# Attention layer 0 of a two-layer encoder: no stores issued from GpSimd, stores one tile later, squares of the softmax sums on ScalarE

## The chip, the cores and the metric

The kernel runs on one core of a Trainium2 chip. A core has five engines that run their own instruction queues side by side: TensorE (PE, matrix products), VectorE (DVE), ScalarE (ACT), GpSimd (POOL) and SyncE (SP, which here only issues DMAs). DMAs can be issued from SP, ACT or POOL. The metric is the device time of one execution in microseconds (us), lower is better.

## The reference

The trunk has 1024 tokens of width 1024 and two layers. Layer 0 is differential attention with 8 heads, layer 1 is multi-head latent attention. Only layer 0's attention is touched here:

```python
def block(qb):
    sc = jnp.einsum('bqhcd,bkhcd->bhcqk', qb, k, preferred_element_type=f32) * scale
    p = jax.nn.softmax(sc, axis=-1)
    p = p[:, :, 0] - lam * p[:, :, 1]
    return jnp.einsum('bhqk,bkhd->bqhd', p.astype(v.dtype), v)
o = _from_blocks(lax.map(block, _to_blocks(q)))
o = _rmsnorm(o, subln_g) * (1.0 - lambda_init)
o = o.reshape(b, s, DA_WIDTH) * jax.nn.silu(z)
return o @ w_out
```

For each head there are two softmaxes, their difference times V, an RMS norm over the 128 values of the head (the "sub-norm"), and a product with a gate silu(z). All is in float32.

## The kernel before

Every float32 product is made of three matrix products of rounded parts: an operand is split into a high part (ACT copies it to the type that TensorE reads) and a low part (DVE or POOL subtracts), and `mm3` issues high x high, high x low and low x high (L178 to L180).

**The stage.** Layer 0's attention runs over 8 heads, two halves of 512 query rows, and four tiles of 128 rows in each half: 64 tiles. For one tile `q_tile` makes two score matrices of 128x1024 (L1157), each with a maximum on DVE (L456) and an exponential with its sum on ACT (L458); the sums of the first softmax of four tiles stand in the four columns of `zz`. DVE then combines the two exponentials (L1163 to L1165). One to two tiles later PE transposes the result (L439), ACT and DVE split it (L441, L442), and `pv` multiplies it with V. Because the combined exponentials are not divided by the first softmax's sum, the sub-norm must know the square of that sum: `subln` (L1236) adds a multiple of `zz` squared to the mean square of the output before the inverse root.

**Work laid beside it.** Between the pieces of a tile `fill` steps a stream of other matrix products (the projections of the next heads, `gen_strips0`, written `acc`). By `FILL0` a tile has five such steps or three. After each step, and once more at the end of each tile, `side.tick()` runs the next entry of a queue of small jobs. A job of `rot_job` (L369) turns one half of a head's q or k by its position: POOL makes two products and a sum (`first_`, `second`, L390 to L394), ACT copies the high part and issues its store (`high`, L398 and L400), POOL makes the low part (`low`, L403), and the low part is stored. `None` entries in the queue space the steps out. `z_done` (L847) makes a gate and stores it.

**The sub-norm.** When a half of a head is through, `head_out` on ACT takes the squares and a scaled copy of the output out of PSUM, and `subln` multiplies by the gate on POOL (L1240). Its `rest` is put on a list, `hooks`, and runs at the end of the next tile (`after_scores` runs the hooks that were there before the tile's last `pv`). `rest` sums the squares with a matrix product against ones (L1247), then has four DVE instructions on 128x4 values (L1250 to L1253), an inverse root on POOL (L174) and a product on POOL (L1255). L1250 and L1252 read two operands from SBUF, L1253 one, L1251 one from SBUF and one from PSUM. `finish` then sends the four factors through DRAM so that they come back as a row on all partitions: a store (L1195), one tile later a load (L1199), one tile after that a product (L1202) and the store of the output (L1203). The store of L1195, that of L1203 and that of the low part (L405) are issued from POOL.

**What sets the order.** A planner arranges the instructions of each engine ahead of time from its own estimate of when each can start, so an instruction can stand on its engine well ahead of its place in the program: L1250, which needs only `zz`, runs before the matrix product that L1251 needs. `in_turn` keeps an instruction in the order of the program, which is done for all of POOL's work here; `behind` keeps one behind the latest instruction that matters on its engine. On the chip each engine works its list from front to back, and an instruction that waits holds those behind it. SP's list holds nearly all loads and stores.

**The end of the stage.** In head 7 the stream is used up, and the first products of the output projection take its place (`extra0`, L1613). They need the outputs of earlier heads from DRAM (`oF`), loaded by SP and split on ACT and POOL (L1518, L1519). The sub-norms of head 7 run from a list of their own, `rests`.

Of the kernel before, what the change touches and what calls it, by code (L numbers as in the profile page):

```python
# [15 lines left out]
AF = mybir.ActivationFunctionType  # L16
ALU = mybir.AluOpType
# [4 lines left out]
P = 128  # L22
# [5 lines left out]
NH = 8  # L28
QL = 384
KVL = 256  # L30
EPS = 1e-6
# [7 lines left out]
ROT = 2  # L39
# [33 lines left out]
GUARD = 2.0 ** 40  # L73
FMAX = 3.4028e38
# [5 lines left out]
def f32v(ap):  # L80
    return ap.bitcast(F32)
# [3 lines left out]
def trunk(ctx: ExitStack, tc: tile.TileContext, A, out):  # L85
    nc = tc.nc
    SP, PE, V, S, G = nc.sync, nc.tensor, nc.vector, nc.scalar, nc.gpsimd
# [47 lines left out]
    oF = [dr.tile([NH, 2, P, HF], F32, name=f"oF{l}") for l in range(2)]  # L135
# [3 lines left out]
    zS = dr.tile([NH, 2, P, HF], F32, name="zS")  # L139
    rS = [[[dr.tile([P, HF], F32, name=f"rS{k}{h}{f}") for f in range(2)] for h in range(NH)] for k in range(2)]  # L140
    hS = [[[dr.tile([2, P, HF], F32, name=f"hS{k}{h}{f}") for f in range(2)] for h in range(NH)] for k in range(2)]
# [29 lines left out]
    def rsqrt(w, n):  # L171

        y = sm.tile([P, n], F32, name="rq_y")
        G.tensor_tensor(out=y, in0=w, in1=mhalf[:, :n], op=ALU.pow)  # L174
        return y
# [9 lines left out]
    def behind(eng):  # L185

        return tc.issue_after(mk[eng]) if eng in mk else nullcontext()

    def in_turn(ins):

        return tc.keep_in_program_order(ins) if mk else ins
# [123 lines left out]
    side = Side()  # L315
# [53 lines left out]
    def rot_job(kind, h, half, eng, raw=None):  # L369

        cs = slice(half * HF, half * HF + HF)
        b = {"raw": raw}
        turn_ = in_turn if eng is G else lambda ins: ins

        def rpt(name):
            return wp.tile([P, HF], F32, name=name, tag="rp", bufs=6)

        def fetch():
            src = b["raw"]
            if src is None:  # L380
                src = rS[kind][h][half]
                b["raw"] = rpt("rp_raw")
                SP.dma_start(b["raw"], src)
            b["sw"] = rpt("rp_sw")
            for q in range(4):
                SP.dma_start(b["sw"][q * 32 : q * 32 + 32], src[(q ^ 1) * 32 : (q ^ 1) * 32 + 32])

        def first_():
            b["r"] = rpt("rp_r")
            turn_(eng.tensor_mul(b["r"], b["raw"], cosT[:, cs]))  # L390

        def second():
            turn_(eng.tensor_mul(b["sw"], b["sw"], sinT[:, cs]))
            turn_(eng.tensor_add(b["r"], b["r"], b["sw"]))  # L394

        def high():
            with behind("S"):
                cp = S.copy(b["sw"].bitcast(F32R), b["r"])  # L398
            with tc.issue_after(cp.ins):
                S.dma_start(hS[kind][h][half][0], b["sw"])  # L400

        def low():
            turn_(eng.tensor_sub(b["raw"].bitcast(F32R), b["r"], b["sw"]))  # L403
            if eng is G:
                in_turn(G.dma_start(hS[kind][h][half][1], b["raw"]))  # L405

        def store():
            if eng is not G:
                SP.dma_start(hS[kind][h][half][1], b["raw"])

        return fetch, first_, second, high, low, store

# [56 lines left out]
    def t3(ap_):  # L469
        return ap_.rearrange("p (t q) -> p t q", t=4)  # L470
# [173 lines left out]
    for f in range(2):  # L644
        fs = slice(f * HF, f * HF + HF)
        spread = PE.matmul(cb[:, fs], ones[0:1, :], crow[0:1, fs], start=True, stop=True).ins
# [158 lines left out]
        store_v(0, *((tp, acc, tt, fh, "tk", 16) if tt < V_LATE else (pg, acc, tt, fh, "ada", 2)))  # L805


    KS, QS, GZ = {}, {}, {}
    parked = []

    def silu_gate(tp, acc):
# [7 lines left out]
    def rot_done(kind, h):  # L819
        def f(acc, half):  # L820
            raw = wp.tile([P, HF], F32, name="rp_raw", tag="rp", bufs=6)
            if kind:
                S.copy(raw, acc)
            else:
                S.mul(raw, acc, SC0)
            fetch, *steps = rot_job(kind, h, half, G, raw)
            fetch()
            side.add(*[None] * ROT, *steps[:2], None, None, *steps[2:4])
        return f

    def load_k(h):
# [15 lines left out]
    def z_done(h):  # L847
        def f(acc, half):
            t = wp.tile([P, HF], F32, name="zth", tag="rp", bufs=6)
            S.activation(t, acc, AF.Tanh, scale=0.5)  # L850
            V.scalar_tensor_tensor(out=t, in0=t, scalar=1.0, in1=acc, op0=ALU.add, op1=ALU.mult)
            SP.dma_start(zS[h, half], t)
            if parked:
                fetch, *steps = rot_job(*parked.pop(0), G)
                side.add(fetch, None, None, *steps[:2], None, None, *steps[2:4])
        return f

    def load_gate(h, half):
# [332 lines left out]
    def finish(o, y, l, h, half, dst, ap_, dgs):  # L1191

        if dst is None and l == 0:
            d_ = dr.tile([HF], F32, name="bc_d", tag="bcd", bufs=4)
            in_turn(G.dma_start(d_.rearrange("(p t) -> p t", p=P), y))  # L1195

            def spread():
                b = ap_.tile([P, HF], F32, name="bc_s", tag="osq", bufs=4)
                SP.dma_start(b, d_[None, :].to_broadcast([P, HF]))  # L1199

                def scale():
                    in_turn(G.tensor_mul(t3(o), t3(o), b.rearrange("p (q t) -> p t q", t=4)))  # L1202
                    in_turn(G.dma_start(oF[l][h, half], o))  # L1203

                hooks.append(scale)

            hooks.append(spread)
            return
        if dst is None:
            b, rb = bcast_rows(ap_, y, "osq", 4)  # L1210

            def scale():
                in_turn(G.tensor_mul(t3(o), t3(o), rb))
                hooks.append(lambda: hooks.append(store))

            def store():
                SP.dma_start(oF[l][h, half], o)

            hooks.append(scale)
            return  # L1220
        rb = bank("z", "rb") if l else Y[1]
        for j in range(4):
            js = slice(j * P, (j + 1) * P)
            S.mul(dgs[:, js], ident, y[:, j : j + 1])
            PE.matmul(rb[:, js], ones, dgs[:, js], start=True, stop=True)
        V.tensor_mul(o, o, rb)
# [9 lines left out]
    def subln(o, sq, zz, half, h, dst):  # L1236


        if dst is None:
            in_turn(G.tensor_mul(o, o, GZ[h][half]))  # L1240
        else:
            V.tensor_mul(o, o, GZ[h][half])

        def rest():
            pt = Y[0] if dst is not None else ssq_at[0] if ssq_at else bank("acc", "ssq")
            for j in range(4):
                PE.matmul(pt[:, j : j + 1], sq[:, j * P : (j + 1) * P], ones[:, 0:1], start=True, stop=True)  # L1247
            w = sm.tile([P, 4], F32, name="sl_w")
            fin = sm.tile([P, 4], F32, name="sl_f")
            V.tensor_mul(fin, zz, zz)  # L1250
            V.scalar_tensor_tensor(out=w, in0=fin, scalar=P * EPS / GUARD ** 2, in1=pt[:, 0:4], op0=ALU.mult, op1=ALU.add)  # L1251
            V.scalar_tensor_tensor(out=fin, in0=fin, scalar=FMAX / GUARD ** 2, in1=w, op0=ALU.mult, op1=ALU.is_ge)  # L1252
            V.tensor_scalar(w, w, 3.0e38, None, op0=ALU.min)  # L1253
            y = rsqrt(w, 4)
            in_turn(G.tensor_mul(y, y, fin))  # L1255
            if dst is not None:
                return lambda: finish(o, y, 0, h, half, dst, None, sq)
            finish(o, y, 0, h, half, None, a0b, sq)

        if dst is None:  # L1260
            (hooks if h < NH - 1 else rests).append(rest)
        else:
            return rest()
# [28 lines left out]
            if kh == 1 and qp % 2 == 1:  # L1292
                c["close"](qp // 2, c["o_"], self.zz)

    tails, hooks = [None, None], []

    def run_tails(fill):

# [184 lines left out]
    class Seven:  # L1483
# [32 lines left out]
        def put(self, raw, hi, lo, eng):  # L1516
            with behind("S"):
                S.copy(hi, raw)  # L1518
            sub = eng.tensor_sub(lo, raw, f32v(hi))  # L1519
            if eng is G:  # L1520
                in_turn(sub)
                self.sub = sub.ins

        def fetch(self, n):
            for h in range(4):
                self.fetch_a(n, h)
                self.fetch_w(n, h)
# [319 lines left out]
    for n, rows, acc, f in ((3, 4, Z, 1), (4, 0, Z, 1), (5, 4, Y, 1), (6, 4, Y, 0)):  # L1847
# [5 lines left out]
        for i in range(4):  # L1853
# [24 lines left out]
            if i == 1 and n == 5:  # L1878
                raws = [[], []]
                with tc.issue_after(w6):  # L1880
                    for k, (tag, nb) in enumerate((("wraw", 2), ("gz", 3))):
                        for f in range(2):
                            raw = wst.tile([P, HF], F32, name="wraw", tag=tag, bufs=nb)
# [225 lines left out]
    for h in range(2):  # L2109
        w = strip1(6 + h)  # L2110
# [481 lines left out]
    def scale(tt, y):  # L2592
        full, early = xs_[tt], tt // 4
        c1, c2_ = halves[early], halves[1 - early]

        def second():
            V.scalar_tensor_tensor(out=full[:, c2_], in0=full[:, c2_], scalar=y, in1=fg[:, c2_], op0=ALU.mult, op1=ALU.mult)
            SP.dma_start(out[tt][:, c2_], full[:, c2_])

        def first_():  # L2600
            S.mul(full[:, c1], full[:, c1], y)
            SP.dma_start(out[tt][:, c1], full[:, c1])

        if tt == NT - 2:
            held.extend((second, first_))
        else:
            second()
            first_()
# [160 lines left out]
```

## Time and profile before

| what | us |
|---|---|
| median of 3 runs | 1430.9 |
| lowest, highest | 1430.05, 1431.73 |
| the profiled execution | 1429.41 |
| its span, from the first to the last instruction | 1427.6 |
| PE, DVE, ACT, POOL busy in it | 1374.6, 1027.2, 733.6, 729.7 |

The profiled execution takes 1429.41 us, of which 1427.6 lie between its first and its last instruction. The last head of the attention of layer 0 ends near 720 us on the span's own clock, and its 64 tiles begin near 220 us. PE's busy time counts the whole pipeline of a matrix product, so PE can be "busy" and still not work at its densest.

### The profile page before, as it was taken

How to read it: one execution, taken by the hardware profiler on the slowest of the kernel's cores; microseconds unless marked ns; L12 is line 12 of the kernel's file. 1: busy time of each engine (PE TensorE's matmuls, PEld its weight loads, DVE VectorE, ACT ScalarE, POOL GpSimd, SP SyncE). 2: the span in 40 equal slices, each digit the busy share in tenths (PEclk: the TensorE clock that was granted, in tenths of full speed). 3: DMA queues.
4: the chain of work that ended last, by engine and by line, in shares of the span. 5: the costliest groups of instructions: out<-in, count | busy, mean ns of one | idle time of the engine just before them, and what ended most of it. 6: DMA issues, size and time to landing. Idle time of an engine off the chain costs nothing.

```text
span 1427.6 us, 20963 instructions
## 1 busy us (share of the span) xinstructions
PE 1374.6 (96%) x7298; PEld 1143.4 (80%) x7298; DVE 1027.2 (72%) x1418; ACT 733.6 (51%) x1332; POOL 729.7 (51%) x600
## 2 busy tenths in 40 slices
PE   8998899999999999999899999999999999999997
PEld 6786678778878778888687788887888888888886
DVE  7699927998887878788777986744656555555684
ACT  5543314556655555665655653334454454555554
POOL 5424440556788685565686332533141263754773
PEclk9999999999999999999999999999999999999999
DMA  9845788777778767765484236488444355665373
GB/s 338 267 123 186 274 221 276 216 228 228 237 226 241 220 208 210 213 194 177 138 312 155 77 81 222 141 279 254 158 121 118 110 152 184 194 219 199 132 262 118
DMA packets 172604, 282.42 MB, mean 198 GB/s; under 512 B 21777, under 2 KB 58769, under 8 KB 172498
## 3 DMA queue, kind: packets, MB, share of 16 engines
q1 hardware_dynamic: 164290, 262.43, 58.9%
q0 software_dynamic: 3600, 10.26, 2.0%
q10 hardware_dynamic: 4608, 8.39, 1.6%
q8 instruction: 57, 0.93, 0.3%
q14 instruction: 49, 0.40, 0.1%
HBM read 182.49 MB, written 86.98 MB: 189 GB/s over the span
## 4 chain that ended last, share of the span: by engine, by line
PE 69%; DVE 13%; issue 5%; DMA 5%; POOL 4%; ACT 3%; SPq 1%; POOLq 0%; ACTq 0%; DVEq 0%
PE s L2383 10%; PE tr L439 6%; PE acc L178 6%; PE acc L180 6%; PE acc L179 6%; PE s L1157 5%; PE pv L178 3%; PE pv L179 3%; PE pv L180 3%; DVE ada L480 2%; DVE sl_f L1250 1%; PE oy L180 1%; PE vps L178 1%; PE oy L179 1%; PE vps L179 1%
## 5 line engine op out<-in xcount | busy, mean ns | idle before, releaser
L441 ACT CAST pth<-tr 128x512 fp32r<-128x512 f32 x256 | 150.5, 588 | 264.7 <-PE tr L439 262.1
L442 DVE TENSOR_TENSOR ptl<-tr,pth 128x512 fp32r<-128x512 f32 x256 | 176.0, 688 | 138.2 <-ACT pth L441 133.6
L456 DVE TENSOR_REDUCE nm<-s 128x1 f32<-128x1024 f32 x192 | 233.6, 1217 | 19.6 <-PE s L1157 10.4
L224 POOL TENSOR_TENSOR wl<-wraw,wh 128x512 fp32r<-128x512 f32 (+2 forms) x65 | 84.2, 1298 | 272.7 <-ACT wh L223 211.1
L458 ACT ACTIVATE e<-s,nm 128x1024 f32<-128x1024 f32 x128 | 143.6, 1122 | 70.5 <-DVE nm L456 70.0
L439 PE MATMUL tr<-ident,e 128*128 128x128 f32 x1024 | 156.7, 275 | 14.6 <-DVE ptl L442 14.3
L439 PEld LDWEIGHTS tr<-ident,e 128*128 128x128 f32 x1024 | 121.3, 141 | 58.4 <-DVE ptl L442 37.3
L178 PE MATMUL pv<-pth,vt 128*128 128x256 f32 x512 | 147.8, 289 | 0.0
L179 PE MATMUL pv<-ptl,vt 128*128 128x256 f32 x512 | 147.6, 288 | 0.0
L180 PE MATMUL pv<-pth,vt 128*128 128x256 f32 x512 | 145.1, 283 | 0.0
L178 PE MATMUL acc<-h0h,wh 128*128 128x512 f32 x264 | 109.5, 415 | 3.8 <-DVE zu L1054 3.4
L180 PE MATMUL acc<-h0h,wl 128*128 128x512 f32 x264 | 105.1, 398 | 0.6 <-POOL wl L224 0.6
L179 PE MATMUL acc<-h0l,wh 128*128 128x512 f32 x264 | 105.7, 400 | 0.0
L178 PEld LDWEIGHTS pv<-pth,vt 128*128 128x128 f32 x512 | 97.7, 191 | 3.0 <-ACT pth L441 0.4
L179 PEld LDWEIGHTS pv<-ptl,vt 128*128 128x128 f32 x512 | 98.1, 192 | 1.8
L180 PEld LDWEIGHTS pv<-pth,vt 128*128 128x128 f32 x512 | 98.1, 192 | 0.4
L1519 POOL TENSOR_TENSOR wol<-wol,woh 128x512 fp32r<-128x512 f32 x56 | 82.3, 1493 | 26.3 <-ACT woh L1518 23.7
L1157 PE MATMUL s<-ks,qa 128*128 128x512 f32 x256 | 85.8, 416 | 8.5 <-DVE e L1165 8.0
L1165 DVE SCALAR_TENSOR_TENSOR e<-s,z,e 128x1024 f32<-128x1024 f32 x64 | 82.2, 1284 | 2.1
L1157 PE MATMUL s<-ks,qb 128*128 128x512 f32 x256 | 83.5, 401 | 0.0
L458 ACT ACTIVATE s<-s,nm 128x1024 f32<-128x1024 f32 x64 | 70.0, 1093 | 8.5 <-DVE nm L456 8.1
L224 POOL TENSOR_TENSOR wl<-zraw,wh 128x512 fp32r<-128x512 f32 (+2 forms) x32 | 46.0, 1444 | 52.0 <-ACT wh L223 48.7
(496 smaller groups left out, 3653.1 us busy)
## 6 DMA issues: line engine op xcount, KB each, us to landing
ada<-in_ada_ss SPq DMA_DIRECT2D x32, 512.0 KB, 5.7
vt<-vS SPq DMA_DIRECT2D x32, 512.0 KB, 5.6
wol<-tS SPq DMA_DIRECT2D x56, 256.0 KB, 5.2
wraw<-in_w_s SPq DMA_DIRECT2D x52, 256.0 KB, 3.5
vS<-v_hl SPq DMA_DIRECT2D x26, 512.0 KB, 6.0
tS<-ob SPq DMA_DIRECT2D x48, 256.0 KB, 2.6
bc_s<-bc_d SPq DMA_DIRECT2D x34, 256.0 KB, 4.0
hS<-rp_sw ACTq DMA_DIRECT2D x32, 256.0 KB, 3.4
```

The costliest lines, as they stand in the source:

```text
L178: PE.matmul(psum, ah, bh, start=first, stop=False, skip_group_check=skip)
L179: PE.matmul(psum, ah, bl, start=False, stop=False, skip_group_check=skip)
L180: mm3.last = PE.matmul(psum, al, bh, start=False, stop=last, skip_group_check=skip).ins
L224: sub = (V if pair_of else G).tensor_sub(l_[:, :n], raw[:, :n], f32v(h_[:, :n]))
L439: transpose_p.last = PE.transpose(tr[:, j, :], p[:, kt * P : (kt + 1) * P], ident).ins
L441: mk["S"] = S.copy(pth[kh][:, :, dst], tr).ins
L442: mk["V"] = V.tensor_sub(ptl[kh][:, :, dst], tr, f32v(pth[kh][:, :, dst])).ins
L456: mk["V"] = V.reduce_max(nm, s_ps, axis=AX.X, negate=True).ins
L458: mk["S"] = S.activation(e, s_ps, AF.Exp, bias=nm, scale=1.0, accum_out=zs).ins
L1157: PE.matmul(s_ps[:, kc * HF : (kc + 1) * HF], src[:, c, ql], KS[h][kc][:, c, :], start=fst, stop=not fst)
L1519: sub = eng.tensor_sub(lo, raw, f32v(hi))
L2383: PE.matmul(s_ps[:, kc * HF : (kc + 1) * HF], lhs, rhs(kc), start=i == 0, stop=i == 4)
```

## The change

Four things are altered, all in layer 0.

- The low part of a turned half is stored by ACT instead of POOL when POOL made it, from an entry of its own in the side queue: two entries after the low part. The pause between `second` and `high` is one entry instead of two.
- The gate's store (heads 1 to 6) is put on `hooks` and so issued at the end of a later tile.
- `finish` for layer 0 goes in five steps: the factors' store from SP one tile after they are made (`put`), then as before load and product, and the output's store from SP one more tile later (`store`).
- In `rest` the two squares of `zz` are made on ACT, with their factors inside the square; the limit of 3e38 is put on the matrix product's sum before the addition; the guard compares with the matrix product's sum in PSUM. Two DVE instructions stay, each with one operand in PSUM.

```diff
         def low():
             turn_(eng.tensor_sub(b["raw"].bitcast(F32R), b["r"], b["sw"]))
-            if eng is G:
-                in_turn(G.dma_start(hS[kind][h][half][1], b["raw"]))
 
         def store():
-            if eng is not G:
-                SP.dma_start(hS[kind][h][half][1], b["raw"])
+            (S if eng is G else SP).dma_start(hS[kind][h][half][1], b["raw"])
...
             fetch, *steps = rot_job(kind, h, half, G, raw)
             fetch()
-            side.add(*[None] * ROT, *steps[:2], None, None, *steps[2:4])
+            side.add(*[None] * ROT, *steps[:2], None, *steps[2:4], None, steps[4])
...
-            SP.dma_start(zS[h, half], t)
+            if 0 < h < NH - 1:
+                hooks.append(lambda: SP.dma_start(zS[h, half], t))
+            else:
+                SP.dma_start(zS[h, half], t)
             if parked:
                 fetch, *steps = rot_job(*parked.pop(0), G)
-                side.add(fetch, None, None, *steps[:2], None, None, *steps[2:4])
+                side.add(fetch, None, None, *steps[:2], None, *steps[2:4], None, steps[4])
...
         if dst is None and l == 0:
             d_ = dr.tile([HF], F32, name="bc_d", tag="bcd", bufs=4)
-            in_turn(G.dma_start(d_.rearrange("(p t) -> p t", p=P), y))
+            rb = []
+
+            def put():
+                SP.dma_start(d_.rearrange("(p t) -> p t", p=P), y)
+                hooks.append(spread)
 
             def spread():
                 b = ap_.tile([P, HF], F32, name="bc_s", tag="osq", bufs=4)
                 SP.dma_start(b, d_[None, :].to_broadcast([P, HF]))
-
-                def scale():
-                    in_turn(G.tensor_mul(t3(o), t3(o), b.rearrange("p (q t) -> p t q", t=4)))
-                    in_turn(G.dma_start(oF[l][h, half], o))
-
+                rb.append(b.rearrange("p (q t) -> p t q", t=4))
                 hooks.append(scale)
 
-            hooks.append(spread)
+            def scale():
+                in_turn(G.tensor_mul(t3(o), t3(o), rb[0]))
+                hooks.append(store)
+
+            def store():
+                SP.dma_start(oF[l][h, half], o)
+
+            hooks.append(put)
             return
...
-            V.tensor_mul(fin, zz, zz)
-            V.scalar_tensor_tensor(out=w, in0=fin, scalar=P * EPS / GUARD ** 2, in1=pt[:, 0:4], op0=ALU.mult, op1=ALU.add)
-            V.scalar_tensor_tensor(out=fin, in0=fin, scalar=FMAX / GUARD ** 2, in1=w, op0=ALU.mult, op1=ALU.is_ge)
-            V.tensor_scalar(w, w, 3.0e38, None, op0=ALU.min)
+            S.activation(w, zz, AF.Square, scale=math.sqrt(P * EPS) / GUARD)
+            S.activation(fin, zz, AF.Square, scale=1.0 / GUARD)
+            V.scalar_tensor_tensor(out=w, in0=pt[:, 0:4], scalar=3.0e38, in1=w, op0=ALU.min, op1=ALU.add)
+            V.scalar_tensor_tensor(out=fin, in0=fin, scalar=FMAX, in1=pt[:, 0:4], op0=ALU.mult, op1=ALU.is_ge)
             y = rsqrt(w, 4)
             in_turn(G.tensor_mul(y, y, fin))
```

The list `hooks` is only made earlier in the program (L808 instead of L1295).

More of the change, by code (lines that the diff above doesn't have):

```diff
@@ L805, in v0_tile @@
         store_v(0, *((tp, acc, tt, fh, "tk", 16) if tt < V_LATE else (pg, acc, tt, fh, "ada", 2)))
-    KS, QS, GZ = {}, {}, {}
+    KS, QS, GZ, hooks = {}, {}, {}, []
     parked = []
@@ L1293, in pv @@
                 c["close"](qp // 2, c["o_"], self.zz)
-    tails, hooks = [None, None], []
+    tails = [None, None]
     def run_tails(fill):
```

## The prediction

> **What bounds the kernel now.** I read the page first, then the busy times by stretch, then the chain of waits, then the groups of DVE's instructions and the timelines around the costliest.
>
> ```profile
> span 1427.6 us, 20963 instructions
> PE 1374.6 (96%) x7298; PEld 1143.4 (80%) x7298; DVE 1027.2 (72%) x1418; ACT 733.6 (51%) x1332; POOL 729.7 (51%) x600
> ```
>
> PE is the bound over the whole span, so only time in which PE stands still can be won. The change lies in the attention of layer 0; the next view gives busy times by stretch (from:to in us, its length, then PE, PEld, DVE, ACT, POOL, the granted clock, the DMA share, GB/s).
>
> ```profile
> 243.00:660.00 417.00, 398.95 (x2278) 335.16 (x2277) 353.90 (x478) 241.77 (x433) 276.66 (x252) 0.99 0.73 219
> ...
> 400.00:420.00 20.00, 16.62 (x90) 13.25 (x89) 18.96 (x22) 9.08 (x16) 15.45 (x15) 1.00 0.67 214
> ...
> 500.00:520.00 20.00, 16.76 (x89) 14.00 (x88) 15.75 (x18) 9.20 (x18) 16.66 (x15) 0.91 0.65 201
> ...
> 620.00:640.00 20.00, 20.00 (x122) 17.47 (x121) 16.33 (x23) 12.71 (x24) 11.69 (x11) 1.00 0.50 149
> ```
>
> From 243 to 660 us PE stands still for 417.00 - 398.95 = 18.05 us, and not evenly: 3.38 and 3.24 us in two stretches of 20 us, nothing in a late one that does the same work. In the stretch from 500 us the granted clock falls to 0.91 as well. The chain of work that ended last (start, us, what) and the groups of DVE name a suspect:
>
> ```profile
> 500.12 4.88 DVE sl_f L1250
> ...
> L1250 DVE TENSOR_TENSOR sl_f<-zz 128x4 f32<-128x4 f32 x16 | 30.2, 1886 | 0.0
> ...
> L1252 DVE SCALAR_TENSOR_TENSOR sl_f<-sl_f,sl_w 128x4 f32<-128x4 f32 x16 | 6.3, 394 | 0.3
> ...
> L1253 DVE TENSOR_SCALAR sl_w<-sl_w 128x4 f32<-128x4 f32 x16 | 5.2, 325 | 0.2
> ```
>
> Four numbers a partition cannot take 1.9 us to square. One line's own view gives the least, the median and the largest duration in ns:
>
> ```profile
> L1250 DVE TENSOR_TENSOR sl_f<-zz x16: 152/1135/4965, 254.3 to 705.4; 128x4 f32<-128x4 f32 x16
> L1252 DVE SCALAR_TENSOR_TENSOR sl_f<-sl_f,sl_w x16: 152/164/981, 277.0 to 722.5; 128x4 f32<-128x4 f32 x16
> L1253 DVE TENSOR_SCALAR sl_w<-sl_w x16: 153/170/1217, 277.2 to 722.8; 128x4 f32<-128x4 f32 x16
> L1251 DVE SCALAR_TENSOR_TENSOR sl_w<-sl_f,ssq x14: 149/159/160, 276.9 to 670.2; 128x4 f32<-128x4 f32 x14
> ```
>
> The same instruction takes 0.152 us or up to 4.965 us; L1251, which reads PSUM beside SBUF, never leaves 0.149 to 0.160. DVE's and POOL's timelines around one of the long ones show what it waits for:
>
> ```profile
> 405.56 4.53 DVE L1250 TENSOR_TENSOR sl_f<-zz 128x4 f32<-128x4 f32 x1
> 410.02 0.68 DVE L442 TENSOR_TENSOR ptl<-tr,pth 128x512 fp32r<-128x512 f32 x1
> ...
> 405.10 1.29 POOL L224 TENSOR_TENSOR wl<-wraw,wh 128x512 fp32r<-128x512 f32 x1
> 406.33 1.29 POOL L1423 TENSOR_TENSOR ot<-ob,ob 128x512 f32<-128x512 f32 x1
> 407.58 1.27 POOL L390 TENSOR_TENSOR rp_r<-rp_raw,cosT 128x512 f32<-128x512 f32 x1
> 408.82 1.25 POOL L393 TENSOR_TENSOR rp_sw<-rp_sw,sinT 128x512 f32<-128x512 f32 x1
> 410.15 1.27 POOL L394 TENSOR_TENSOR rp_r<-rp_r,rp_sw 128x512 f32<-128x512 f32 x1
> ```
>
> POOL runs four instructions without a gap (each starts before the one ahead has ended), and L1250 ends at 410.09 in the first gap, between 410.07 and 410.15. So DVE's small instruction on SBUF is shut out by POOL's for as long as POOL runs without a gap, and L442, which PE needs, stands behind it. **PE pays** (in brackets, idle time and what ended it):
>
> ```profile
> 410.75 0.65 PE L439 MATMUL tr<-ident,e 128*128 128x128 f32 x4 [2.40 <-DVE ptl L442]
> ...
> 507.35 0.66 PE L439 MATMUL tr<-ident,e 128*128 128x128 f32 x4 [3.24 <-DVE ptl L442]
> ```
>
> **The change part by part.** *The squares.* L1250, L1252 and L1253 hold DVE for 30.2 + 6.3 + 5.2 = 41.7 us; at their least durations it would be 16 x (0.152 + 0.152 + 0.153) = 7.3, so 34.4 us are waiting. All three go. The two DVE instructions that stay read one operand from PSUM, as L1251 does, and I cost them at its 0.159. How much of 34.4 us reaches PE: of the wait of 4.53 us PE stood still 2.40, of that of 4.96 us 3.24, shares of 0.53 and 0.65. Small waits are hidden better, so 0.65 x 34.4 = 22.4 is an upper end, the 18.05 us of PE's idle time is another, and a share of 0.2 (7 us) the lower. I take 18: the idle time falls nearly to nothing, as in the late stretch, and the slow clock behind some gaps goes with it. Less DVE work proper, 16 x (0.152 + 0.153) = 4.9 us, I count as 1 us.
>
> The Trainium skill, SBUF — State Buffer, section "SBUF: two separate sides", says that DVE and GpSimd share a port pair under an exclusive lock, that a DVE instruction with two SBUF inputs meets it, and that the loser waits out the other's whole instruction. By that rule alone one wait ends after one POOL instruction, 1.3 us, and L1250 would hold DVE for at most 16 x (0.152 + 1.3) = 23.2 us, 7 less than its row has; the same share of PE's time would make this term -14 and the sum 1417. The trace differs: up to 4.965 us in one wait, so POOL keeps the pair from one instruction to the next. On PSUM operands rule and L1251's row agree.
>
> *ACT.* It gets 24 stores and 32 squares. The nearest rows are the store of the high part from ACT's queue and a small exponential:
>
> ```profile
> L400 ACTq DMA_DIRECT2D hS<-rp_sw  x32: 326/326/363, 128.0 to 650.4; - x32
> ...
> L1139 ACT ACTIVATE lp<-lp 128x2 f32<-128x2 f32 x1 | 0.2, 203 | 2.0 <-DVE lp L1138 2.0
> ```
>
> 24 x 0.326 + 32 x 0.203 = 14.3 us on an engine that is busy 241.77 of 417 us. Bounds: nothing, since PE-bound tiles leave ACT waiting, and 0.65 x 14.3 = 9.3. I take 2, nearer the bottom, as ACT has 175 us free. Then the waits: a store on ACT waits for POOL's low part, and behind it stand the exponentials and the copies that PE's transposes need. This pair of rows shows how late POOL can be:
>
> ```profile
> 365.25 0.62 ACT L398 CAST rp_sw<-rp_r 128x512 fp32r<-128x512 f32 x1 [0.86 <-POOL rp_r L394]
> ...
> 375.19 1.29 POOL L403 TENSOR_TENSOR rp_raw<-rp_r,rp_sw 128x512 fp32r<-128x512 f32 x1
> ...
> ACT rp_sw L398 <- POOL rp_r L394: 5.0, 4, 1.9
> ```
>
> The low part ended 376.48 - 365.87 = 10.6 us after the high part. The store comes three entries after `high`; at five entries a tile and some 7.5 us a tile (417 us over 55 combines) that is 4.5 us. But the planner places it by its own estimate of POOL, and where ACT already waits for POOL (last row), it waited 5.0 us in four places, 1.9 at most. `high` moves one entry up, which can lengthen these. I take 1 us, bounds 0 and 13 (below).
>
> *POOL and SP.* POOL loses its DMA issues:
>
> ```profile
> L405 POOL DMA_DIRECT2D hS<-rp_raw x24 | 14.2, 594 | 8.4 <-POOL rp_raw L403 8.4
> L1195 POOL DMA_DIRECT2D bc_d<-rq_y x15 | 9.1, 608 | 6.0 <-POOL rq_y L1255 4.8 <-PE tr L439 0.8 <-DMA gz<-zS 0.4
> L1203 POOL DMA_DIRECT2D oF<-o x15 | 8.8, 586 | 6.0 <-POOL o L1202 5.2 <-DMA wol<-tS 0.4 <-DMA qa<-hS 0.4
> ...
> L480 DVE CUSTOM_DVE_ANT_0 ada<-ada,c,vec x24: 1267/1286/2314, 119.1 to 362.4; 128x1024 f32<-128x1024 f32 x24
> ```
>
> That is 32.1 us of work and 20.4 us of gaps before it, hidden now since POOL is free for 140 us of the 417: 0. The gaps were also what let DVE in: the sums of L480 keep two SBUF operands and rise from 1.267 to 2.314 us where they meet POOL. Fewer gaps could cost them up to 1 us in each of a dozen places before 362 us; I take 0, with 3 us on PE as the bound. SP gets 30 issues of some 0.3 us and loses its waits for the landing of the factors. No row shows PE waiting for a load in the stage, and the loads are several tiles ahead: 0.
>
> *The end of the stage.* There SP stood at the factors' load until they had landed, and everything else stood behind it:
>
> ```profile
> 677.71 0.32 SPq L1199 DMA_DIRECT2D bc_s<-bc_d  x1
> ...
> 682.16 1.55 POOL L1202 TENSOR_TENSOR o<-o,bc_s 128x512 f32<-128x512 f32 x1 [6.90 <-DMA bc_s<-bc_d]
> ...
> 686.08 0.72 PE L180 MATMUL oy<-woh,oal 128*128 128x512 f32 x1 [2.15 <-POOL oal L1519]
> ```
>
> With store, load and product each a tile apart, the splits (L1519) no longer stand behind a product that waits 6.90 us, and PE's 2.15 us go: -2. The output of head 7's first half is stored later and its load holds SP at the end; PE has a backlog there: 0, bound +3.
>
> **The sum:** -18 - 1 + 2 + 1 - 2 = -18 us. The profiled execution took 1429.41 us (its span and 1.8 around it), so 1411.4; the median of the runs lies 1.5 higher, so 1412.9: **1413**.
>
> **The rivals.** *Half is taken over.* When the waits are gone, the next late input (ACT's copies, L480, ACT's own queue) takes part of the gap: a share of 0.35 of 34.4 is 12, less 1, plus 5 for ACT, is -8, or 1423. For it speaks that L480 keeps its two SBUF operands; against it the late stretch without any idle time.
>
> *ACT waits for POOL's low part* (the other side: slower). If each store stood three entries after `high` and POOL stayed as late as now, ACT would be held; by the pair above 10.6 - 4.5 = 6 us in the worst case, and at 0.8 us in each of 24 stores 20 us over all, which at 0.65 costs PE 13. With 9 us for ACT's added work and 3 for L480 that is +25 against -18 - 1 - 2 = -21: +4, or 1435. It decides from about 15 us of PE's time lost to ACT's holds. For it: the store waits on an engine that feeds PE. Against it: POOL gets 32.1 us freer, and ACT's waits for POOL are 5.0 us now. The Trainium skill, TensorE: Matmul & The Clock Gate, section "Architectural detail: the array is 16× 32×32, not 1× 128×128", states that ACT's queue is strictly first in, first out; that is what this rival rests on, and no run yet shows such a store.
>
> *It doesn't do what it says*: the instructions that stay are shut out too, or the squares wait on ACT. L1251's 0.160 at most speaks against it. Then the time stays, 1429 to 1432.
>
> **How the numbers follow.** The forecast, 1404 to 1421, 0.62; half taken over, 1421 to 1428, 0.15; better than the forecast (the upper end 22.4 and 4 at the stage's end), below 1404, 0.04; no change 0.09; slower 0.10. About 0.2%, 3 us, is what a measurement of this kernel can tell from no change, so faster is 0.81, same 0.09, slower 0.10. The range from 1402 to 1429 holds the forecast, the half and the best case's edge.
>
> **What would show it.** L1250 to L1253 gone, two DVE instructions of 0.16 us in their place, with no long ones; PE idle between 243 us and the stage's end below 6 us instead of 18; no granted clock of 0.91 in 20 us; no POOL wait of 7 us near 680. Wrong: ACT stores with waits of several us, transposes waiting for ACT's copies, POOL waiting longer for ACT, or L480 above 2.3 us.

## The result and the profile after

The changed kernel takes 1425.69 us (median of 13 runs), the kernel before 1430.53 us beside it: a ratio of 0.9968, 95% interval 0.9957 to 0.9979. It is faster by 4.8 us (4.6 by the ratio) where 18 were forecast, and lies inside the forecast range near its slow end. The profiled execution took 1427.42 us.

Lines of the changed kernel are a few off those of before: L436 is PE's transpose, L438 and L439 its split on ACT and DVE, L453 and L455 maximum and exponential, L406 the store of the low part, L1208 the product of `finish`, L1257 to L1260 the squares and the two DVE instructions left. The page and the busy times by stretch:

```profile
span 1425.6 us, 20940 instructions
PE 1373.9 (96%) x7298; PEld 1145.8 (80%) x7298; DVE 987.6 (69%) x1386; ACT 738.5 (52%) x1364; POOL 699.0 (49%) x546
```
```profile
243.00:660.00 417.00, 400.67 (x2287) 340.64 (x2285) 320.05 (x452) 246.11 (x460) 246.36 (x203) 0.98 0.75 221
...
400.00:420.00 20.00, 17.71 (x94) 14.59 (x93) 14.22 (x20) 11.90 (x23) 14.20 (x13) 0.91 0.83 240
...
460.00:480.00 20.00, 16.86 (x86) 13.97 (x86) 12.45 (x20) 11.04 (x22) 12.62 (x12) 0.91 0.78 222
...
520.00:540.00 20.00, 17.54 (x97) 14.90 (x96) 12.71 (x20) 9.20 (x18) 6.04 (x6) 0.91 0.75 234
...
560.00:580.00 20.00, 17.35 (x93) 14.64 (x93) 11.69 (x17) 9.99 (x18) 15.03 (x13) 0.91 0.77 219
```

DVE and POOL got the relief that was worked out: DVE is busy 39.6 us less, POOL 30.7 us less. But PE still stands still for 417.00 - 400.67 = 16.3 us between 243 and 660 us, where it was 18.05, and in four stretches of 20 us the clock falls to 0.91 (before it did so in two). Neither DVE nor POOL is busy throughout in them. The durations of the sub-norm's small instructions (least, median, largest in ns) and the list of waits say what went and what came:

```profile
L1259 DVE SCALAR_TENSOR_TENSOR sl_w<-ssq,sl_w x14: 142/161/163, 278.5 to 669.5; 128x4 f32<-128x4 f32 x14
...
L1260 DVE SCALAR_TENSOR_TENSOR sl_f<-sl_f,ssq x14: 137/147/149, 278.8 to 670.4; 128x4 f32<-128x4 f32 x14
```
```profile
ACT s L455 <- POOL rp_raw L403: 16.7, 4, 5.5
...
ACT pth L438 <- POOL rp_raw L403: 5.4, 2, 3.6
...
ACT e L455 <- POOL rp_raw L403: 4.2, 1, 4.2
...
ACT rp_raw L820 <- POOL rp_raw L403: 2.6, 1, 2.6
```

The long DVE instructions are gone: nothing above 0.163 us. In their place ACT waits 16.7 + 5.4 + 4.2 + 2.6 = 28.9 us (in total, times, longest) for POOL's low part. The trace books these waits to the compute instruction that stands behind the store. ACT's and POOL's timelines around the longest show it:

```profile
453.72 0.62 ACT L398 CAST rp_sw<-rp_r 128x512 fp32r<-128x512 f32 x1 [1.12 <-POOL rp_r L394]
...
456.47 0.58 ACT L438 CAST pth<-tr 128x512 fp32r<-128x512 f32 x1
462.13 0.34 ACTq L406 DMA_DIRECT2D hS<-rp_raw  x1
462.52 1.09 ACT L455 ACTIVATE s<-s,nm 128x1024 f32<-128x1024 f32 x1 [5.47 <-POOL rp_raw L403]
```
```profile
455.49 1.30 POOL L1247 TENSOR_TENSOR o<-o,gz 128x512 f32<-128x512 f32 x1 [1.81 <-ACT o L1241]
456.74 1.54 POOL L1208 TENSOR_TENSOR o<-o,bc_s 128x512 f32<-128x512 f32 x1
458.25 1.27 POOL L1428 TENSOR_TENSOR ob<-ob 128x512 f32<-128x512 f32 x1
459.59 1.29 POOL L1430 TENSOR_TENSOR ot<-ob,ob 128x512 f32<-128x512 f32 x1
460.83 1.26 POOL L403 TENSOR_TENSOR rp_raw<-rp_r,rp_sw 128x512 fp32r<-128x512 f32 x1
```
```profile
463.76 0.16 DVE L1163 RECIPROCAL z<-z 128x1 f32<-128x1 f32 x1 [3.61 <-ACT s L455]
463.84 0.14 DVE L1260 SCALAR_TENSOR_TENSOR sl_f<-sl_f,ssq 128x4 f32<-128x4 f32 x1
```
```profile
464.12 0.47 PE L178 MATMUL acc<-h0h,wh 128*128 128x512 f32 x1 [3.14 <-DVE sl_f L1260]
...
464.65 0.40 PE L180 MATMUL acc<-h0h,wl 128*128 128x512 f32 x1
...
465.35 0.62 PE L180 MATMUL acc<-h0h,wl 128*128 128x512 f32 x1
```

POOL makes the low part in the order of the program, behind four other instructions; it ends at 462.09. The store stands on ACT from 457.05, and the exponential behind it starts only at 462.52, though its scores were there. DVE's next step waits for its sum, L1260 stands behind that step, and PE waits 3.14 us for L1260, which now reads the matrix product's bank that PE wants to reuse. Then the clock is halved (its row reads 0.50 from 466 to 468 us) and products take 0.62 us.

This happens five times. Behind the holds of 4.2, 4.9, 5.5, 4.4 and 3.6 us PE stands still for 2.06, 2.29, 3.14, 2.46 and 2.65 us, together 12.6 of its 16.3 us, and each time a stretch of slow clock follows. The other three holds (1.8, 1.9 and 2.6 us) leave no PE gap over 1.3 us.

### The profile page after: what moved, and what is told of

Read it like the earlier page. It is cut to its first block, busy times and chain, and to the rows that moved or that the text cites. A ratio compares the mean times of both kernels' runs of the same rounds, so it can differ in the third digit from the quotient of the medians.

```text
span 1425.6 us, 20940 instructions
## 1 busy us (share of the span) xinstructions
PE 1373.9 (96%) x7298; PEld 1145.8 (80%) x7298; DVE 987.6 (69%) x1386; ACT 738.5 (52%) x1364; POOL 699.0 (49%) x546
## 4 chain that ended last, share of the span: by engine, by line
PE 68%; DMA 8%; DVE 7%; POOL 6%; ACT 4%; issue 4%; SPq 2%; ACTq 0%; POOLq 0%; DVEq 0%
PE s L2390 10%; PE tr L436 6%; PE acc L178 6%; PE acc L180 6%; PE acc L179 6%; PE s L1157 6%; PE pv L178 4%; PE pv L179 4%; PE pv L180 4%; PE vps L178 1%; PE vps L180 1%; PE zacc L180 1%; PE zacc L178 1%; PE vps L179 1%; PE zacc L179 1%
## 5 line engine op out<-in xcount | busy, mean ns | idle before, releaser
L439 DVE TENSOR_TENSOR ptl<-tr,pth 128x512 fp32r<-128x512 f32 x256 | 176.0, 688 | 155.7 <-ACT pth L438 150.8
L438 ACT CAST pth<-tr 128x512 fp32r<-128x512 f32 x256 | 150.3, 587 | 247.3 <-PE tr L436 236.8
L453 DVE TENSOR_REDUCE nm<-s 128x1 f32<-128x1024 f32 x192 | 233.5, 1216 | 22.3 <-PE s L1157 13.3
L455 ACT ACTIVATE e<-s,nm 128x1024 f32<-128x1024 f32 x128 | 143.6, 1122 | 53.3 <-DVE nm L453 48.1
L436 PE MATMUL tr<-ident,e 128*128 128x128 f32 x1024 | 156.9, 276 | 7.2 <-DVE ptl L439 6.8
L436 PEld LDWEIGHTS tr<-ident,e 128*128 128x128 f32 x1024 | 122.5, 142 | 48.8 <-DVE ptl L439 26.4
L1165 DVE SCALAR_TENSOR_TENSOR e<-s,z,e 128x1024 f32<-128x1024 f32 x64 | 82.2, 1284 | 2.1
L455 ACT ACTIVATE s<-s,nm 128x1024 f32<-128x1024 f32 x64 | 69.9, 1093 | 23.0 <-POOL rp_raw L403 16.7
```

Of the source, the lines that this page charges most:

```text
L436: transpose_p.last = PE.transpose(tr[:, j, :], p[:, kt * P : (kt + 1) * P], ident).ins
L438: mk["S"] = S.copy(pth[kh][:, :, dst], tr).ins
L439: mk["V"] = V.tensor_sub(ptl[kh][:, :, dst], tr, f32v(pth[kh][:, :, dst])).ins
L453: mk["V"] = V.reduce_max(nm, s_ps, axis=AX.X, negate=True).ins
L455: mk["S"] = S.activation(e, s_ps, AF.Exp, bias=nm, scale=1.0, accum_out=zs).ins
```

## The experiments

All changes are in the same three places. The kernel before, run beside each set, had medians of 1430.0, 1430.0 and 1431.5 us; behind each time stands the ratio to it with its 95% interval. Where an edit changes the side queue, the like edit to the second `side.add` (in `z_done`) is not shown; where POOL stores, `store` is as in the kernel before.

**Which queue stores the low part.** First SP in place of ACT, then POOL as before (with the old spacing), all else as changed.

```diff
-            (S if eng is G else SP).dma_start(hS[kind][h][half][1], b["raw"])
+            SP.dma_start(hS[kind][h][half][1], b["raw"])
```

> The changed kernel, but the low part made by POOL is stored from SP, at the same entry of the side queue. Theory A (the changed kernel's ACT is held some 29 us by stores that wait for POOL's low part, and PE stands still in six places for 2.2 to 3.3 us because of it): those holds go, PE idle from 243 to 660 us falls from 16 us to under 6, the granted clock stays at 1.00 there, and the time falls by 8 to 16 us against the changed kernel, to 1410 to 1418. Theory B (other late inputs take the gap whatever queue stores: POOL's turn of the halves, the shorter pause before the high part): the time stays within 3 us of the changed kernel's 1425.7. Theory C (SP is now the one that is held, and loads come late): slower than the changed kernel, with PE or POOL waiting for DMAs.

Measured: 1427.9 us, 0.9985 (0.9974 to 0.9995): not theory A. The time alone, 2.2 us above the changed kernel, fits B as well as C; the next run and `pause_only` speak against B, and the trace for C. SP's waits, its queue and PE in that run:

```profile
SPq L406 <- POOL rp_raw L403: 71.6, 16, 10.8
```
```profile
521.84 0.33 SPq L865 DMA_DIRECT2D wraw<-in_w_s  x1
533.30 0.32 SPq L406 DMA_DIRECT2D hS<-rp_raw  x1
...
535.21 1.32 SPq L841 DMA_DIRECT2D qa<-hS  x2
```
```profile
540.34 2.00 PE L1157 MATMUL s<-ks,qa 128*128 128x512 f32 x4 [1.90 <-issue]
```

SP stood 71.6 us at these stores, once from 522 to 533 us, and the load of q behind it was issued at 535.2, just ahead of the scores that need it, which PE began only at 540.3. The hold moved from one queue to the other. How much of PE's time that costs, this trace shows only in part: this wait of 1.90 us is the only one of PE that the view of L841, the loads of q, names, and the other gaps over 2 us (2.41, 2.09 and 2.10 us) are ended by DVE and ACT.

```diff
         def low():
             turn_(eng.tensor_sub(b["raw"].bitcast(F32R), b["r"], b["sw"]))
+            if eng is G:
+                in_turn(G.dma_start(hS[kind][h][half][1], b["raw"]))
...
-            side.add(*[None] * ROT, *steps[:2], None, *steps[2:4], None, steps[4])
+            side.add(*[None] * ROT, *steps[:2], None, None, *steps[2:4])
```

> The changed kernel with one part undone: the low part is stored by POOL right behind the instruction that makes it, and the side queue has its old spacing; squares, gate store and the five steps of finish stay as changed. Theory A: no holds on ACT, so 1410 to 1418, as with SP; POOL is 14 us busier, which PE does not see. Theory B: within 3 us of 1425.7 if the gap is taken by other inputs; if it was the shorter pause before the high part, as theory A.

Measured: 1412.3 us, 0.9877 (0.9860 to 0.9894): theory A. POOL, which makes the low part, never waits long for itself (0.4 us at most at these stores).

**The squares by themselves**, on the kernel before, and then the changed kernel without them (the two edits mirror each other):

```diff
-            V.tensor_mul(fin, zz, zz)
-            V.scalar_tensor_tensor(out=w, in0=fin, scalar=P * EPS / GUARD ** 2, in1=pt[:, 0:4], op0=ALU.mult, op1=ALU.add)
...
+            S.activation(w, zz, AF.Square, scale=math.sqrt(P * EPS) / GUARD)
+            S.activation(fin, zz, AF.Square, scale=1.0 / GUARD)
...
```

> The kernel before with the squares alone: two squares on ACT and two DVE instructions with a PSUM operand in place of four DVE instructions on SBUF. Theory A: 34 us of DVE waiting go and nothing holds ACT, so the 18 us forecast for this part come, less 1 to 3 us for ACT's squares: 1412 to 1418. Theory D (my share of 0.52 of DVE's waits is too high, because PE catches up behind a gap): 1422 to 1427. It also gives the worth of the other parts by difference.

> The changed kernel with the squares undone (four DVE instructions as before); stores on ACT and SP stay as changed. Theory A: DVE waits and ACT holds both, 1438 to 1446, slower than before by 8 us or more. Theory D (DVE's waits cost PE little): 1427 to 1433. Without POOL's DMA issues, DVE finds fewer gaps between POOL's instructions, so the first of the four waits as long as before or longer, 30 us or more.

Measured: the squares alone 1412.2 us, 0.9877 (0.9860 to 0.9894), theory A. Without them 1429.6 us, 0.9995 (0.9983 to 1.0007), which is theory D's range, and my number for DVE's wait was a miss:

```profile
L1257 DVE TENSOR_TENSOR sl_f<-zz 128x4 f32<-128x4 f32 x16 | 6.3, 396 | 0.0
...
L1260 DVE TENSOR_SCALAR sl_w<-sl_w 128x4 f32<-128x4 f32 x16 | 6.2, 389 | 0.3
L1259 DVE SCALAR_TENSOR_TENSOR sl_f<-sl_f,sl_w 128x4 f32<-128x4 f32 x16 | 4.8, 300 | 0.3
```

The same three instructions take 17.3 us here, 41.7 in the kernel before. Why they wait less here was not settled; a shift of their place against POOL's runs without a gap would do it, but no run tests that. So the squares are worth 17.8 us in one kernel (1430.0 - 1412.2) and 3.9 in the other (1429.6 - 1425.7).

**Is it the wait, the issues or the spacing?** The next two answer it: a store on ACT that waits for nothing on POOL (it stores the high part a second time, so the result is not right), and POOL's store with the changed kernel's shorter pause.

```diff
-            (S if eng is G else SP).dma_start(hS[kind][h][half][1], b["raw"])
+            (S if eng is G else SP).dma_start(hS[kind][h][half][1], b["sw"] if eng is G else b["raw"])
```

> The changed kernel, but the store that ACT issues for the low part takes its data from the high part (ACT's own result), so it waits for nothing on POOL; the second half of hS gets the wrong data, all instructions, issues and spacings stay. Theory A (the wait in ACT's queue is what costs): 1410 to 1415, and no PE gap over 2 us that an ACT instruction ends. Theory B (ACT's 24 issues, or the shorter pause before the high part): 1422 to 1428.

Measured: 1406.5 us, 0.9829 (0.9808 to 0.9850). The same instructions and issues, without the wait, are 19.2 us faster than the changed kernel, even more than theory A had. This run also lets go of the low part's buffer sooner; `act_behind` below, with the right data, gives 15.8 of the 19.2. From 243 to 660 us PE stands still for 7.3 us, and the clock is never slow:

```profile
243.00:660.00 417.00, 409.67 (x2390) 349.46 (x2389) 337.00 (x476) 260.29 (x486) 255.61 (x210) 1.00 0.77 230
```

The second is made from `low_on_pool`:

```diff
-            side.add(*[None] * ROT, *steps[:2], None, None, *steps[2:4])
+            side.add(*[None] * ROT, *steps[:2], None, *steps[2:4], None)
```

> The kernel with the low part stored by POOL right behind the low part (1412.3), but with the changed kernel's spacing of the side queue: one empty entry before the high part instead of two. Theory A: 1411 to 1415, as the wait of the high part for POOL's sum grows by a few us at most. Theory B: 1418 or more, with ACT's waits for L394 above the 7.5 us of the kernel it is made from, by 8 us or more.

Measured: 1403.4 us, 0.9811 (0.9793 to 0.9829). The shorter pause is no cost but a gain of 8.9 us; neither theory had that. The two kernels' ACT waits for POOL's sum, and ACT and PE at the longest in `low_on_pool`:

```profile
ACT rp_sw L398 <- POOL rp_r L394: 7.5, 2, 4.9
```
```profile
ACT rp_sw L398 <- POOL rp_r L394: 14.5, 9, 2.8
```
```profile
348.96 0.62 ACT L398 CAST rp_sw<-rp_r 128x512 fp32r<-128x512 f32 x1 [4.86 <-POOL rp_r L394]
350.00 1.11 ACT L458 ACTIVATE e<-s,nm 128x1024 f32<-128x1024 f32 x1 [0.42 <-ACT rp_sw L398]
```
```profile
351.25 1.22 PE L1160 MATMUL s<-ks,qa 128*128 128x512 f32 x2 [3.83 <-ACT e L458]
```
```profile
340.00:360.00 20.00, 16.17 (x80) 13.30 (x79) 12.34 (x18) 8.93 (x19) 9.92 (x9) 0.83 0.77 223
```

With the shorter pause ACT waits twice as long in all, but never more than 2.8 us at once. With the longer one a single wait of 4.86 us stops PE for 3.83 us, and the clock falls to 0.83 of 20 us, another 3.4 us: 7.2 of the 8.9 us in one place. Here one long hold costs more than nine short ones.

**A later place for the store.** Twice by the list of hooks, a tile later, on ACT and on SP:

```diff
+            if eng is G:
+                hooks.append(lambda: S.dma_start(hS[kind][h][half][1], b["raw"]))
...
```

> The changed kernel, but the store of the low part by ACT is put on the list of hooks and so issued at the end of a later tile, some 7 us after its entry. Theory A: POOL is through by then, ACT's waits for L403 fall from 29 us to under 5, 1409 to 1415. Theory B: within 3 us of 1425.7. A third outcome: the raw buffers are held a tile longer, and ACT or POOL waits for a buffer: above 1415 with new waits for DMAs of hS.

> The same with the store issued by SP at the end of a later tile. Theory A (a queue that stands at the store holds what is behind it, whichever queue it is): SP's waits for L403 fall from 71.6 us to under 15, loads come in time, 1409 to 1415. Theory C (SP has too much to issue): stays above 1420, with PE waiting for loads of q and k.

Measured: 1419.9 us, 0.9924 (0.9905 to 0.9942), and 1420.4 us, 0.9929 (0.9911 to 0.9946). The first falls between theories A and B; the second stands at the edge of C in time, but PE's weight load waits for a load of q in one place only, 1.2 us. The waits for L403 shrank and did not go, ACT's in the first from 28.9 to 18.6 us, SP's in the second from 71.6 to 28.8:

```profile
ACT s L458 <- POOL rp_raw L403: 15.0, 4, 4.7
...
ACT e L458 <- POOL rp_raw L403: 3.6, 1, 3.6
```
```profile
SPq L407 <- POOL rp_raw L403: 28.8, 9, 6.7
```

The program's place had hardly moved the store: counted in ACT's rows of the traces it stands 2.3 rows behind the high part's store on average in the changed kernel, and 2.6 here, where the program asks for a whole tile. My reading is that the planner puts it where it believes POOL to be through. So the place was forced, once at the old entry and once a tile later:

```diff
+            if eng is G:
+                with behind("S"):
+                    S.dma_start(hS[kind][h][half][1], b["raw"])
```

> The changed kernel, but the ACT store of the low part is kept behind the ACT instruction that stands last in the program at that point, so that the planner can't place it earlier; it now stands 4.2 rows behind the high part's store on ACT on average, instead of 2.3. Theory A1 (the planner places the store by its own estimate of POOL, and so ahead of where the program asks for it; a place later in the queue takes the holds away): 1406 to 1415, ACT's waits for L403 under 10 us instead of 29. Theory A2 (even the asked place is too early): above 1415, with waits left in proportion.

> The same, with the store a tile later in the program by the list of hooks: 6.0 rows behind on average. Theory A1 and A2 both: ACT's waits for L403 under 5 us, 1403 to 1410. If it stays above 1415 without such waits, a buffer that is held longer is the cost, and POOL or ACT waits for a DMA of hS.

Measured: 1409.9 us, 0.9852 (0.9837 to 0.9867), and 1414.6 us, 0.9886 (0.9869 to 0.9903). In the first one wait for L403 is left:

```profile
ACT pth L442 <- POOL rp_raw L403: 1.9, 1, 1.9
```

Two rows further back in the queue are worth 15.8 us: theory A1. The tile later was to be better still, lies outside its range and is 4.7 us slower, with the waits for L403 all but gone as well (2.1 us). Most of that is the cost that its expectation named for a time above 1415, a buffer held longer:

```profile
244.41 0.69 DVE L390 TENSOR_TENSOR rp_r<-rp_raw,cosT 128x512 f32<-128x512 f32 x1 [2.96 <-DMA hS<-rp_raw]
245.02 0.68 DVE L446 TENSOR_TENSOR ptl<-tr,pth 128x512 fp32r<-128x512 f32 x1
```
```profile
245.76 0.66 PE L443 MATMUL tr<-ident,e 128*128 128x128 f32 x4 [2.58 <-DVE ptl L446]
```

DVE stands 2.96 us until a store of the low part has landed, PE's transposes wait 2.58 us for the split behind it, and the clock from 240 to 260 us falls to 0.91, another 1.8 us. POOL waits once for such a landing too, 12.6 us. `act_behind` has no wait for these stores.

**The stores of `finish`, and no pause at all**, on the kernel before with the squares. First the shorter pause:

```diff
-            side.add(*[None] * ROT, *steps[:2], None, None, *steps[2:4])
+            side.add(*[None] * ROT, *steps[:2], None, *steps[2:4], None)
```

> The kernel before with the squares and the shorter pause alone: all stores as before. If the five steps of finish and the gate's store are worth nothing here too, as between 1412.3 and 1412.2 without the shorter pause: 1401 to 1406, the same as 1403.4. If they are worth something once PE has no other gaps: 1406 to 1412.

Then none:

```diff
-            side.add(*[None] * ROT, *steps[:2], None, None, *steps[2:4])
+            side.add(*[None] * ROT, *steps[:4], None, None)
```

> The same with no empty entry at all before the high part. If the gain of 9 us from the shorter pause comes from the high part and all behind it being ready sooner: the same or better, 1398 to 1404. If it was one place in the queue where ACT stood for 5 us (347 us in one kernel, 406 in the other), then any shift removes or restores it: 1403 to 1414, and ACT's waits for L394 rise above 20 us, as the high part is asked for right behind the sum.

Measured: 1409.1 us, 0.9842 (0.9825 to 0.9858), in the second of its two ranges, and 1420.3 us, 0.9927 (0.9912 to 0.9942), slower than both of its ranges, though the waits rose as the second one said. ACT's waits for POOL's sum are in order:

```profile
ACT rp_sw L398 <- POOL rp_r L394: 24.5, 13, 3.9
```
```profile
ACT rp_sw L398 <- POOL rp_r L394: 45.1, 18, 5.9
```

The new `finish` and the gate's later store are thus worth 5.7 us with the shorter pause (1409.1 against 1403.4; 4.4 by the ratios, as the two ran in different sets) and nothing without it (1412.2 against 1412.3). With no pause ACT is held 45.1 us and 11 us are lost: PE stands 3.69 us behind a hold of 5.86 us and 3.02 behind one of 5.15. `pause_only` beats all: the changed kernel with the low part's store left on POOL, 1403.4 us, 22 us faster than the changed kernel.

## Why the prediction was wrong

| from | to | us |
|---|---|---|
| before | squares alone | 1430.0 to 1412.2: -17.8 |
| squares alone | and `finish`, gate | 1412.2 to 1412.3: 0 |
| that | and the shorter pause | 1412.3 to 1403.4: -8.9 |
| that | and 24 issues on ACT without the wait | 1403.4 to 1406.5: +3.1 |
| that | and the wait: the changed kernel | 1406.5 to 1425.7: +19.2 |

- *The squares: right in size and mechanism, and in part by luck.* I had -18, -1 and part of +2 for ACT; alone they gave -17.8, a share of 17.8 / 34.4 = 0.52, the one I took. The DVE instructions with a PSUM operand are never shut out (0.163 us at most). But the idle time did not fall "nearly to nothing". From the first combine (L1165) to the end of the last, before and with the squares alone:

```profile
232.10:709.20 477.10, 453.56 (x2578) 380.27 (x2577) 401.06 (x546) 281.05 (x503) 304.24 (x277) 0.99 0.72 215
```
```profile
231.80:691.90 460.10, 447.57 (x2578) 379.31 (x2577) 365.39 (x515) 285.46 (x535) 307.48 (x278) 0.99 0.74 223
```

  The stage is 17.0 us shorter, PE's idle time 23.5 - 12.5 = 11.0, and by the rows of 20 us the clock gives another 2. The rest, some 4 us, comes out of time in which PE counts as busy, which the prediction held could not be won.
- *ACT's added work: about right.* 14.3 us of it, priced at +2; 24 issues and what goes with them cost 3.1, the squares' own part is inside the -17.8.
- *ACT's waits: this step failed.* "I take 1 us, bounds 0 and 13 (below)." It was 19.2, beyond my upper bound. Two reasons. I let the planner answer for it: it "places it by its own estimate of POOL", and I read ACT's 5.0 us of waits for L394 as a sign that the store would not be held either. The runs show the reverse for the low part: the store stands 2.3 rows behind on ACT, while at the longest hold POOL has four instructions ahead of L403. And I priced the hold at 0.65 of its length, taken from DVE's waits; here 28.9 us of holds cost 19.2, a share of 0.66. The length was wrong, I had 20 us, in the rival alone; that the rate came out is luck, for mine counted PE's idle time alone. The same stretch, changed kernel and `act_no_wait`:

```profile
233.20:706.20 473.00, 451.82 (x2575) 382.53 (x2574) 364.26 (x515) 285.61 (x534) 274.43 (x227) 0.98 0.73 217
```
```profile
231.80:686.30 454.50, 444.75 (x2575) 378.35 (x2574) 364.96 (x515) 285.95 (x534) 275.85 (x227) 1.00 0.76 226
```

  Of the 18.5 us between them 21.2 - 9.8 = 11.4 are idle time, a share of 0.40 of the holds, and the rows of 20 us give some 7 for the slow clock, a term that the prediction did not have here.
- *The rival on the other side had the right mechanism, and the other rival the right number, by luck.* "ACT waits for POOL's low part" happened in full, at 28.9 us instead of 20. It did not end slower than before since the shorter pause, which I counted as a possible loss, brought 8.9. The time fell into the band of "half is taken over" (1421 to 1428), but alone the squares gave their full share. The Trainium skill, TensorE: Matmul & The Clock Gate, section "Architectural detail: the array is 16× 32×32, not 1× 128×128", calls ACT's queue strictly first in, first out; the trace agrees, with an exponential 5.47 us behind a store it has nothing to do with.
- *The pause: wrong sign.* The waits of the high part did grow, 7.5 to 14.5 us, but the longest shrank, and with it went most of the gain. How much it brings hangs on the rest: 8.9 us here, 1412.2 - 1409.1 = 3.1 on the kernel before with the squares.
- *SP and the gate's store: 0 was right* by the pair without the shorter pause, and up to 5.7 us better by the other.
- *POOL's fewer gaps: right.* L477, the sum with two SBUF operands, rises to 2.309 us at most, as before (2.314).
- *The end of the stage: not as forecast.* The product no longer waits for its row of factors, as said. Yet PE's idle time from 660 to 720 us went from 60.00 - 53.09 = 6.9 to 60.00 - 53.42 = 6.6 us, not down by 2: POOL waits for ACT and PE there instead (11.7 and 8.8 us in two places). The clock of the stretch rose from 0.97 to 1.00, which is worth 1.8 us; no run takes this part alone, so what it brought stays open.

```profile
660.00:720.00 60.00, 53.09 (x307) 43.89 (x306) 39.71 (x60) 38.14 (x69) 35.93 (x33) 0.97 0.57 179
```
```profile
660.00:720.00 60.00, 53.42 (x315) 43.51 (x314) 39.31 (x57) 38.73 (x73) 35.44 (x30) 1.00 0.54 171
```
```profile
POOL o L1247 <- ACT o L1241: 13.7, 2, 11.7
POOL oal L1526 <- PE s L1157: 8.8, 1, 8.8
```

The differences in the table hold in the order in which they stand; the squares are worth 3.9 us when ACT is held, as `no_squares` shows. Whether the planner takes POOL to be faster than it is, and why, was not looked into.

## What to carry to other kernels

In this kernel a store that waits for another engine did best on the queue of the engine that makes its data, or far enough behind it in the other queue's actual list: ask what stands behind it and who waits for that, and look up the place in the planned list, not in the program. Price holds one by one, by the gap that each leaves on PE and the slow clock behind it, not by their sum: PE had no gap over 1.0 us behind nine waits of up to 2.8 us and stood 3.83 us behind one of 4.9. The length alone does not decide: a hold of 3.6 us left a gap of 2.65 us in the changed kernel, one of 3.9 us left 0.56 in `squares_pause`. A small instruction on two SBUF operands beside a busy POOL can take thirty times its own length (4.965 against 0.152 us), and moving one operand to PSUM or the work to ACT took that away here.

## What the runs showed of the hardware that was not expected

PE's clock is halved after gaps that are short: behind 3.14 us of idle time products go from 0.40 to 0.62 us, and the stretch of 20 us around it has a mean clock of 0.91, some 3.6 us at half speed. Behind the gap of 3.83 us the mean is 0.83, about twice that. So these gaps cost their own length and 1.8 to 3.4 us more. Gaps of 2.06 to 2.65 us were followed by slow clock as well, four times in the changed kernel; but after one of 2.40 us in the kernel before, at 411 us, the row stayed at 1.00. The Trainium skill, TensorE: Matmul & The Clock Gate, section "What's actually happening", gives a window of 3.4 us and half the clock after an idle one; the gaps here, of 2.06 to 3.14 us, are under that, so less than a whole window sufficed.

DVE's wait beside POOL lasts as long as POOL runs without a gap, up to 4.965 us through four instructions. How much of it there is differs between kernels with the same instructions: 34.4 us of such waits in the kernel before, 17.3 - 7.3 = 10.0 in `no_squares`.
